# Hybrid decoder step: the first feed-forward block on its own, totals two blocks ahead, a fifth PSUM bank

## The chip, the cores and the metric

The kernel runs on one core of a Trainium2 chip. The metric is the time of one execution on the device in microseconds (us), as the median of three runs; a profile of one further execution shows where its time goes. Engines are TensorE (PE, with PEld for its weight loads), VectorE (DVE), ScalarE (ACT), GpSimd (POOL) and the queue that starts the loads (SP). Each engine works through its own queue in order; semaphores tie them together.

## The reference, cut to what matters

One inference step of a one-layer recurrent decoder for 256 prompt tokens and 8 x 4 sample tokens, 288 columns in all, with the width D = 2048. Three mixers run in parallel (RG-LRU, GLA, mLSTM), then an output projection; what the change touches is behind it:

```python
sh1, sc1, gt1, sh2, sc2, gt2 = [m[:, None, :] for m in jnp.split(mod, 6, axis=-1)]
...
x = x + gt1 * mix                                  # mix = merged @ P['w_out']
xn = rmsnorm(x, P['g_norm2']) * (1.0 + sc2) + sh2  # the second norm
x = x + gt2 * (jnp.square(jax.nn.relu(xn @ P['w_ff1'])) @ P['w_ff2'])
...
y = rmsnorm(x, g_final)
```

`w_ff1` is 2048 x 8192 and `w_ff2` 8192 x 2048, both f32. All tensors are f32.

## The kernel before, in words

Activations lie feature-major: 16 tiles of 128 features by 288 columns. The weights are streamed from HBM in pieces of 128 x 1024 f32 (512 KB).

**Feed-forward.** The hidden width is cut into 8 parts `hb`. A part takes four blocks of the first layer (`ff1`, weight `wf1`, two PSUM banks each) and four of the second (`ff2`, weight `wf2`, four banks each, summed up over the parts in `facc`, that is slots 6 and 7). `ff2(hb - 1)` follows `ff1(hb)`. A block has four pieces `g`, and each piece costs TensorE 24 matmuls: the f32 weight is split into two f16 halves, hi and lo, the activation likewise, and three of the four products are summed. So FF has 64 blocks, 256 steps `s` (one piece each) and 6144 matmuls.

The split needs a power of two for each block, so that f16 holds the halves. For a piece and a block (`class Block`):

- `fetch(i)` starts the load of piece `i` into one of 11 places. A place is free again when the piece that lay there is converted.
- `scan` squares the piece on ScalarE and sums it (L229, output to a scrap tile `con`, the sum in `sums`).
- `total` (one small TensorE matmul, L233, into a bank `px`) and `scale` (five tiny VectorE instructions, L198 to L201 and L238) make the power of two out of the block's four sums.
- `convert` writes hi, on ScalarE for the pieces listed in `by_act` (L242), else on VectorE (L244), and lo always on VectorE (L245). Both go to a tile `pair`, of which there are six.
- `multiply` issues the matmuls (L256). In a block's last piece they go bank by bank, and behind each bank stands its `evac`: in `ff1` a relu and a square on ScalarE (L1852, L1853); in `ff2` one VectorE instruction that adds the bank to `facc` (L1867), a copy on ScalarE for the first part, and in the last two parts also the gated residual (`resid`, L1757 to L1762). What reads a bank last sets it free; the pool `pm` has four.

`hidden_rows`, `hidden_total` and `hidden_part` do the same split for the hidden activations of a part: a total on TensorE, and four pairs of a ScalarE (L1844) and a VectorE instruction (L1845).

**What sets the order.** `feed_forward` writes the order out by hand, and `in_order` fixes it on TensorE, ScalarE and VectorE. Step `s` scans piece `s + 8`, scales the next block if `s % 4` is 1, converts piece `s + 3`, fetches `s + 14`, multiplies `s`, and issues the next block's total if `s % 4` is 0. Ahead of step 0 it fetches 11 pieces and scans 8. The first eight pieces belong to two blocks taken in turn, so that each norm tile serves twice as many matmuls. What stands outside `in_order` is placed by a scheduler.

**The second norm.** The output projection's last block ends with `resid` and the squares for the norm (L592); `scaled` multiplies x by the conditioning scale on GpSimd (slots `xf`), and `rstd_of` forms the reciprocal root (L601 on TensorE, L622 to L626 on VectorE with L624 on ScalarE). Then come 16 norm tiles `k`, outside `in_order`: the product with the root (L1813, VectorE), hi by ScalarE (L1814 for the prompt columns, L1817 for the sample columns), the sample columns' shift and lo (L1816, L1819, GpSimd from the third tile on), and lo for the prompt (L1818, VectorE). They use two row buffers in turn.

Beside the feed-forward, conditioning weights (`wada`) for `gt2` are prepared and multiplied (L404 to L412, and L426 on TensorE); `every` says at which steps.

Of the kernel before, what the change touches and what calls it, by code (L numbers as in the profile page):

```python
# [14 lines left out]
P = 128  # L15
D = 2048
KT = D // P
NP = 256
# [36 lines left out]
def trunk(ctx, tc, io):  # L55
# [151 lines left out]
    def in_order():  # L207
# [4 lines left out]
        for i in traced[n:]:  # L212
# [3 lines left out]
            if i.engine in (mybir.EngineType.PE, mybir.EngineType.Activation, mybir.EngineType.DVE):  # L216
                queued[i.engine] = i

    class Block:

        def __init__(self, w, blk, g0, width, act, back, evac, by_act):
# [24 lines left out]

        def multiply(self, g, hi, lo, ms, kks):
            if self.ps is None:
                self.ps = [pm.tile([P, 512], F32, tag="mm", name=nm("mm")) for _ in range(self.nm_t)]
            hi, lo = (t_.rearrange("p (k m) -> p k m", k=self.kg) for t_ in (hi, lo))  # L250
            for m in ms:
                for kk in kks:
                    k = self.kg * g + kk
                    xh, xl = self.act(k)
                    for i, (a, x) in enumerate(((hi, xh), (hi, xl), (lo, xh))):
                        pace["last"] = T.matmul(self.ps[m][:, :N], a[:, kk, m * P:(m + 1) * P], x, start=k == 0 and i == 0,  # L256
                                                stop=k == 4 * self.kg - 1 and i == 2)
# [1544 lines left out]
                scaled(i)  # L1802
        run(stream(io["wout"], b, act_m, KT, ev_o))
    every("")
    scaled(3)
    rs = rstd_of(pss)
    x16 = big.tile([P, 2, KT, N], F16, tag="xh", name="x16")
    with tc.high_priority():
        for k in range(KT):
            f = row(("ar", "mr")[k % 2])  # L1810
            E = V if k < 2 else G
            h, l, sh = x16[:, 0, k, :], x16[:, 1, k, :], mod[:, SH2, k, 0:1]
            V.tensor_tensor(out=f, in0=xf[k // 8][:, k % 8, :], in1=rs, op=ALU.mult)  # L1813
            S.activation(h[:, 0:NP], f[:, 0:NP], AF.Identity, bias=sh)  # L1814
            fs = f[:, NP:N].rearrange("p (b t) -> p b t", b=NB)
            E.tensor_tensor(out=fs, in0=fs, in1=mod[:, SH2, k, 1:9].unsqueeze(2).to_broadcast([P, NB, TS]), op=ALU.add)  # L1816
            S.activation(h[:, NP:N], f[:, NP:N], AF.Copy)  # L1817
            V.scalar_tensor_tensor(l[:, 0:NP], f[:, 0:NP], sh, h[:, 0:NP], ALU.add, ALU.subtract)  # L1818
            E.tensor_tensor(out=l[:, NP:N], in0=f[:, NP:N], in1=h[:, NP:N], op=ALU.subtract)  # L1819


    facc = (slot(6), slot(7))
    pss = None

    h = slot(2)
    hx = [big.tile([P, 2, 8, N], F16, tag=f"s{i}", name=nm("hx")) for i in range(2)]
# [20 lines left out]
    def ff1(hb):  # L1847
        for b in range(4):
            def ev(m, p, c, b=b):
                i = 2 * b + m  # L1850
                r = t288()
                S.activation(r, p, AF.Relu, scale=c)  # L1852
                S.activation(h[:, i, :], r, AF.Square, accum_out=hof[hb % 2][:, 8 + i:9 + i])  # L1853
            yield Block(io["wf1"], 4 * hb + b, 0, 256, lambda k: (x16[:, 0, k, :], x16[:, 1, k, :]), lambda: xback, ev, (1,))

    def ff2(hb):
        x = hx[hb % 2]
        for b in range(4):
            def ev(m, p, c, b=b):
                k = 4 * b + m  # L1860
                a = facc[k // 8][:, k % 8, :]
                if hb == 0:
                    S.activation(a, p, AF.Copy, scale=c)
                    return
                x = x2[k // 8][:, k % 8, :]
                if hb < 7:
                    V.scalar_tensor_tensor(a, p, c, a, ALU.mult, ALU.add)  # L1867
# [10 lines left out]
            yield Block(io["wf2"], b, 4 * hb, 512, lambda k: (x[:, 0, k, :], x[:, 1, k, :]), lambda: hback[hb][0], ev, (0, 1, 2))  # L1878

    blocks, after = [], {}  # L1880
    for hb in range(9):
        if hb < 8:
# [16 lines left out]
    def fetch(i):  # L1899
        if i >= total:  # L1900
            return
        j = i % 11
        if j < 2:
            t = big8[:, 1024 * j:1024 * j + 1024]
        elif j < 6:
            t = bigx[:, 1024 * (j - 2):1024 * (j - 1)]
        elif j < 9:
            t = wp.tile([P, 1024], F32, tag="raw", name=nm("raw"), bufs=3)
        else:
            t = big3[:, 1024 * (j - 9):1024 * (j - 8)]  # L1910
        b, g = order[i]
        Q.dma_start(t, b.w[b.blk, b.g0 + g])
        raws[i] = t
# [13 lines left out]
    def multiply(s):  # L1927
        b, g = order[s]
        ms, kks = range(b.nm_t), range(b.kg)
        if s < 8:  # L1930
            if s % 2 == 0:
                for kk in kks:
                    for i in (s, s + 1):
                        order[i][0].multiply(order[i][1], *pairs[i], ms, (kk,))
        elif g < 3:
            b.multiply(g, *pairs[s], ms, kks)
        else:
            for m in ms:
                b.multiply(g, *pairs[s], (m,), kks)
                b.evac(m, b.ps[m][:, :N], b.c)  # L1940
        if s in (6, 7):
            for m in ms:
                b.evac(m, b.ps[m][:, :N], b.c)
        del pairs[s]

    def feed_forward():

        with in_order():
            for i in range(11):
                fetch(i)  # L1950
            for i in range(8):
                scan(i)
                if i > 5:
                    blocks[i - 6].total()
                    blocks[i - 6].scale()
            for i in range(3):
                convert(i)
                fetch(11 + i)
        for s in range(total):
            if s == total - 33:  # L1960
                drain("gt1")
            if s == total - 16:
                tail.update(pss=longp(), ssum=row("gc"))
            b = s // 4 + 1
# [12 lines left out]

    slots.update(ids=(9, None, "st"), n=0)
    high.update(ids=(None,))
# [130 lines left out]
```

## Time and profile before

| | |
|---|---|
| median of three runs | 1926.03 us (1923.81 to 1926.28) |
| the profiled execution | 1925.75 us, span 1924.0 us |
| TensorE busy | 1850.7 us, 96% of the span |
| VectorE, ScalarE, GpSimd busy | 1280.6 us (67%), 1114.8 us (58%), 178.1 us (9%) |
| mean granted TensorE clock | 0.992 |
| HBM traffic | 403.56 MB read, 218 GB/s read and written over the span |
| feed-forward on TensorE | 1110.33 us to about 1910 us |

A row of a timeline gives the start in the span, the length, the engine, the line of the kernel and the operation with its tiles, then how often, and in brackets the idle time before it with what ended it. Rows of waits give who waited for whom, the sum, the number and the longest. Windows give the busy time of each engine named, the granted clock as a share of full speed, the share of the DMA engines that was busy, and GB/s. TensorE's matmuls overlap, so a group of them appears some 0.15 us longer than the distance to the next one.

### The profile page before, as it was taken

The numbers are of one execution on the slowest core, as the hardware profiler recorded it, in microseconds if no ns is written. First come the engines' busy times: TensorE is split into PE (matmuls) and PEld (weight loads), VectorE is DVE, ScalarE is ACT, GpSimd is POOL, SyncE is SP. The second block draws the span as 40 slices with busy tenths as digits, with TensorE's granted clock in tenths as the row PEclk, the third lists the DMA queues.
The fourth block names the chain that finished last, engine by engine and source line by source line (L and its number), as shares of the span: only waits on it lengthen the run. The fifth ranks groups of instructions, "written<-read, shape, count | busy, mean of one in ns | idle before, by whom it ended". The sixth has DMA issues, their size and how long they took to land.

```text
span 1924.0 us, 38831 instructions
## 1 busy us (share of the span) xinstructions
PE 1850.7 (96%) x15874; PEld 1622.3 (84%) x15874; DVE 1280.6 (67%) x2290; ACT 1114.8 (58%) x1861; POOL 178.1 (9%) x251
## 2 busy tenths in 40 slices
PE   8999999999999999999999789998999999999987
PEld 7998888999999999999999667777777777777765
DVE  4677746545684457776468578666867776767686
ACT  5333464445455344566367468967777767575654
POOL 0002100001141000011110620000000000000002
PEclk9999999999999999999999989999999999999999
DMA  9998756547744369856796665574565555555441
GB/s 386 399 369 309 249 200 235 208 156 275 253 155 163 134 202 309 295 184 238 285 358 255 249 241 183 160 249 145 173 211 183 165 187 164 187 164 188 145 130 50
DMA packets 113442, 422.90 MB, mean 220 GB/s; under 512 B 11808, under 2 KB 12096, under 8 KB 110064
## 3 DMA queue, kind: packets, MB, share of 16 engines
q1 hardware_dynamic: 97040, 361.04, 54.2%
q0 software_dynamic: 11472, 42.79, 6.4%
q10 hardware_dynamic: 4752, 16.60, 2.1%
q8 instruction: 124, 2.03, 0.4%
q14 instruction: 54, 0.44, 0.1%
HBM read 403.56 MB, written 16.81 MB: 218 GB/s over the span
## 4 chain that ended last, share of the span: by engine, by line
PE 75%; DVE 11%; ACT 9%; issue 3%; DMA 2%; SPq 0%; DVEq 0%; POOL 0%; ACTq 0%; POOLq 0%
PE mm L169 39%; PE mm L256 25%; ACT con L229 4%; PE pa L365 3%; DVE pair L245 3%; ACT pair L242 2%; PE px L169 2%; DVE lo L162 1%; DVE s L1867 1%; DMA raw<-win 1%; DVE pair L244 1%; DVE s L1757 1%; PE pa L426 1%; ACT hi L160 0%; DVE s L793 0%
## 5 line engine op out<-in xcount | busy, mean ns | idle before, releaser
L256 PEld LDWEIGHTS <-pair 128*128 128x128 f16 x6144 | 597.7, 98 | 192.9 <-issue 34.6
L160 ACT ACTIVATE hi<-raw 128x1024 fp32r<-128x1024 f32 x272 | 287.0, 1057 | 411.7 <-PE mm L169 254.5
L162 DVE TENSOR_TENSOR lo<-raw,hi 128x1024 fp32r<-128x1024 f32 x272 | 334.9, 1233 | 250.5 <-ACT hi L160 229.3
L169 PE MATMUL mm<-xh,hi 128*128 128x288 f32 x1440 | 428.8, 301 | 4.0 <-ACT xh L711 1.6
L169 PE MATMUL mm<-xl,hi 128*128 128x288 f32 x1440 | 423.4, 297 | 0.0
L169 PE MATMUL mm<-xh,lo 128*128 128x288 f32 x1440 | 412.3, 296 | 2.0 <-DVE lo L162 1.9
L256 PE MATMUL mm<-hx,pair 128*128 128x288 f16 x3072 | 386.2, 287 | 27.5 <-DVE s L1867 21.5
L256 PE MATMUL mm<-x,pair 128*128 128x288 f16 x3072 | 381.8, 287 | 4.2 <-DVE pair L244 2.5
L169 PEld LDWEIGHTS mm<-xh,hi 128*128 128x128 f32 x1440 | 269.9, 188 | 15.8 <-issue 8.1
L169 PEld LDWEIGHTS mm<-xl,hi 128*128 128x128 f32 x1440 | 270.3, 188 | 1.4
L169 PEld LDWEIGHTS mm<-xh,lo 128*128 128x128 f32 x1440 | 266.2, 188 | 4.9 <-DVE lo L162 2.9
L169 PE MATMUL mm<-s,hi 128*128 128x288 f32 x1280 | 254.1, 298 | 1.1 <-DVE s L1762 0.7
L169 PEld LDWEIGHTS mm<-s,hi 128*128 128x128 f32 x1280 | 203.2, 189 | 5.2 <-issue 2.9
L169 PE MATMUL mm<-s,lo 128*128 128x288 f32 x640 | 179.9, 297 | 1.6 <-DVE lo L162 1.0
L245 DVE SCALAR_TENSOR_TENSOR pair<-s,sums,pair 128x1024 f16<-128x1024 f32 x94 | 120.5, 1288 | 38.5 <-ACT pair L242 37.2
L245 DVE SCALAR_TENSOR_TENSOR pair<-xl,sums,pair 128x1024 f16<-128x1024 f32 x93 | 119.5, 1291 | 30.5 <-ACT pair L242 29.1
L169 PEld LDWEIGHTS mm<-s,lo 128*128 128x128 f32 x640 | 117.6, 189 | 2.3 <-DVE lo L162 2.1
L245 DVE SCALAR_TENSOR_TENSOR pair<-raw,sums,pair 128x1024 f16<-128x1024 f32 x69 | 88.3, 1283 | 27.9 <-ACT pair L242 26.9
L229 ACT ACTIVATE con<-s 128x1024 bf16<-128x1024 f32 x94 | 98.4, 1047 | 6.2 <-DMA s<-wf 5.2
L229 ACT ACTIVATE con<-xl 128x1024 bf16<-128x1024 f32 x93 | 97.2, 1046 | 3.2 <-DMA xl<-wf 2.3
L1852 ACT ACTIVATE t<-mm,sums 128x288 f32<-128x288 f32 x64 | 31.8, 498 | 89.6 <-PE mm L256 89.6
L610 POOL TENSOR_TENSOR row<-row,t 128x288 f32<-128x288 f32 x11 | 12.7, 1153 | 762.1 <-ACT t L608 761.5
(516 smaller groups left out, 2131.2 us busy)
## 6 DMA issues: line engine op xcount, KB each, us to landing
raw<-win SPq DMA_DIRECT2D x192, 512.0 KB, 4.6
s<-wf SPq DMA_DIRECT2D x94, 512.0 KB, 4.0
xl<-wf SPq DMA_DIRECT2D x93, 512.0 KB, 3.9
raw<-wf SPq DMA_DIRECT2D x69, 512.0 KB, 4.0
s<-wq SPq DMA_DIRECT2D x20, 1024.0 KB, 9.8
raw<-wout SPq DMA_DIRECT2D x32, 512.0 KB, 5.7
s<-wada SPq DMA_DIRECT2D x13, 1024.0 KB, 7.5
ag<-wada POOLq DMA_DIRECT2D x12, 1024.0 KB, 9.3
```

The lines of the kernel that those rows point to most:

```text
L160: pace["hi"] = S.activation(hi, raw, AF.Copy)
L162: pace["lo"] = V.tensor_tensor(out=lo, in0=raw, in1=hi.bitcast(F32), op=ALU.subtract)
L169: pace["last"] = T.matmul(ps, w[:, kk, ms], x, start=k == k0 and i == 0, stop=k == kt - 1 and i == 2)
L229: pace["hi"] = S.activation(junk, raw, AF.Square, accum_out=self.of[:, g:g + 1])
L242: pace["hi"] = S.activation(hi, raw, AF.Copy, scale=self.u)
L244: V.tensor_scalar(hi, raw, self.u, None, ALU.mult)
L245: pace["lo"] = V.scalar_tensor_tensor(lo, raw, self.u, hi, ALU.mult, ALU.subtract)
L256: pace["last"] = T.matmul(self.ps[m][:, :N], a[:, kk, m * P:(m + 1) * P], x, start=k == 0 and i == 0, stop=k == 4 * self.kg - 1 and i == 2)
L365: pace["prod"] = T.matmul(ps[32 * j:32 * j + 32, h * w // 4:(h + 1) * w // 4], stat(k), v[:, j], start=k == 0 and h == 0, stop=k == kt - 1 ...
L426: pace["prod"] = T.matmul(ps[32 * j:32 * j + 32, a:a + 256], c, v[:, j], start=q == i == n == 0, stop=q == KT // each - 1 and n == 1, skip ...
L1757: V.scalar_tensor_tensor(x[:, 0:NP], z[:, 0:NP], mod[:, kind, k, 0:1], x[:, 0:NP], ALU.mult, ALU.add)
L1852: S.activation(r, p, AF.Relu, scale=c)
```

## The change

It has five parts.

1. The first block runs alone. Its four pieces are loaded into places that the output projection leaves (three `raw` tiles and one `hi` tile), scanned, totalled and scaled ahead of the norm. The norm's tiles move into `feed_forward`, into `in_order`, four ahead of each of the first four steps, with a third row buffer, and three of the 16 products go to GpSimd.
2. From then on a step converts piece `s + 3` first, fetches `s + 14` and scans piece `s + 10`. The total of block `s // 4 + 2` is issued at `s % 4 == 2`; its scale stands where it stood, with the block's first conversion.
3. Other pieces are converted by ScalarE: `by_act` is (0,) for `ff1`, was (1,), and (0, 2, 3) for `ff2`, was (0, 1, 2). `hidden_part` comes one step later.
4. Every fifth bank is taken from the pool `pi`; the sum for the last norm moves to `pa`.
5. In the last part but one the residual is computed by GpSimd (`half_resid`), in three instructions a tile; VectorE only adds the bank to `facc`.

```diff
+    def bank():
+
+        taken["n"] += 1
+        return longp() if taken["n"] % 5 == 0 else pm.tile([P, 512], F32, tag="mm", name=nm("mm"))
...
-                self.ps = [pm.tile([P, 512], F32, tag="mm", name=nm("mm")) for _ in range(self.nm_t)]
+                self.ps = [bank() for _ in range(self.nm_t)]
...
-    with tc.high_priority():
-        for k in range(KT):
-            f = row(("ar", "mr")[k % 2])
...
+    def second_norm(k):
+
+        f = row(("ar", "mr", "gc")[k % 3])
+        E = V if k < 2 else G
+        h, l, sh = x16[:, 0, k, :], x16[:, 1, k, :], mod[:, SH2, k, 0:1]
+        (G if k % 4 == 3 and k < 15 else V).tensor_tensor(out=f, in0=xf[k // 8][:, k % 8, :], in1=rs, op=ALU.mult)
+        S.activation(h[:, 0:NP], f[:, 0:NP], AF.Identity, bias=sh)
...
+        V.scalar_tensor_tensor(l[:, 0:NP], f[:, 0:NP], sh, h[:, 0:NP], ALU.add, ALU.subtract)
...
-            yield Block(io["wf1"], 4 * hb + b, 0, 256, lambda k: (x16[:, 0, k, :], x16[:, 1, k, :]), lambda: xback, ev, (1,))
+            yield Block(io["wf1"], 4 * hb + b, 0, 256, lambda k: (x16[:, 0, k, :], x16[:, 1, k, :]), lambda: xback, ev, (0,))
+
+    def half_resid(x, a, k):
+
+        G.tensor_scalar(a[:, 0:NP], a[:, 0:NP], mod[:, GT2, k, 0:1], None, ALU.mult)
+        s = a[:, NP:N].rearrange("p (b t) -> p b t", b=NB)
+        G.tensor_tensor(out=s, in0=s, in1=mod[:, GT2, k, 1:9].unsqueeze(2).to_broadcast([P, NB, TS]), op=ALU.mult)
+        G.tensor_tensor(out=x, in0=x, in1=a, op=ALU.add)
...
-                        resid(x, a, GT2, k)
+                        half_resid(x, a, k)
...
-                after[s + 1 + 2 * i] = lambda hb=hb, i=i: hidden_part(hb, i)
+                after[s + 2 + 2 * i] = lambda hb=hb, i=i: hidden_part(hb, i)
...
-    order = [(blocks[i % 2], i // 2) for i in range(8)] + [(b, g) for b in blocks[2:] for g in range(4)]
+    order = [(b, g) for b in blocks for g in range(4)]
...
+        if i == 3:
+            t = wp.tile([P, 1024], F32, tag="hi", name=nm("raw"), bufs=3)
+        elif i < 4 or j > 7:
+            t = wp.tile([P, 1024], F32, tag="raw", name=nm("raw"), bufs=3)
...
+    first = {0: ((), (1,), ()), 1: ((4, 5), (2,), ()), 2: ((6, 7), (3,), (1,)), 3: ((8, 9), (4, 5, 6), ()),
+             4: ((10, 11, 12), (7,), ()), 5: ((13, 14, 15), (), (2,)), 6: ((16,), (8, 9), (3,))}
...
+            scans, converts, totals = first.get(s) or ((s + 10,), (s + 3,), (s // 4 + 2,) if s % 4 == 2 else ())
             with in_order():
-                scan(s + 8)
-                if s > 4 and s % 4 == 1 and b < len(blocks):
-                    blocks[b].scale()
-                convert(s + 3)
-                fetch(s + 14)
+                if s < 4:
+                    with tc.high_priority():
+                        for k in range(4 * s, 4 * s + 4):
+                            second_norm(k)
+                for i in converts:
+                    b, g = order[min(i, total - 1)]
+                    if g == 0 and i < total:
+                        b.scale()
+                    convert(i)
+                    fetch(i + 11)
+                for i in scans:
+                    scan(i)
                 multiply(s)
-                if s > 3 and s % 4 == 0 and b < len(blocks):
-                    blocks[b].total()
+                for b in totals:
+                    if b < len(blocks):
+                        blocks[b].total()
...
+    with in_order():
+        for i in range(4):
+            fetch(i)
+        for i in range(4):
+            scan(i)
+        for i in range(4, 12):
+            fetch(i)
+        blocks[0].total()
+        blocks[0].scale()
+        convert(0)
+    scaled(3)
+    rs = rstd_of(pss)
```

The table `first` gives, for the first seven steps, the pieces to scan, the pieces to convert and the blocks to total.

How the engines' queues change is shown at three places. In the rows a tile's number tells one buffer from another; `s`, `xl` and `raw` are places of loaded pieces, `row` the norm's row buffers, `x` (left of the arrow) the normed activations.

ScalarE at the end of the output projection, before: the last conversions of `wout`, the four squares for the norm, the table for the root, then a first scan.

```order
L160 ACTIVATE hi_12541<-raw_12540 128x1024
L592 ACTIVATE t_1748_12556<-s_1535_11145 128x288
...
L592 ACTIVATE t_1756_12631<-s_1535_11145 128x288
L1788 ACT_TABLE_LOAD
L1788 ACTIVATE warm_12560<-row_11151 128x1
L229 ACTIVATE con,sums_12815<-s_1783_12798 128x1024
L624 ACTIVATE rsc_12674<-t_1758_12672,eps 128x9
L229 ACTIVATE con,sums_12817<-s_1783_12798 128x1024
L1814 ACTIVATE x_12678<-row_12679,mod 128x256
L1814 ACTIVATE x_12678<-row_12686,mod 128x256
```

After:

```order
L160 ACTIVATE hi_12541<-raw_12540 128x1024
L236 ACTIVATE con,sums_12683<-raw_12675 128x1024
...
L236 ACTIVATE con,sums_12683<-raw_12681 128x1024
L599 ACTIVATE t_1748_12556<-s_1535_11145 128x288
...
L1795 ACTIVATE warm_12560<-row_11151 128x1
L249 ACTIVATE pair_12703<-raw_12675,sums_12683 128x1024
L631 ACTIVATE rsc_12714<-t_1773_12712,eps 128x9
L1821 ACTIVATE x_12666<-row_12718,mod 128x256
```

The four scans of the first block (now L236) stand ahead of the squares, and its first conversion ahead of the root; the scans that stood among the norm's tiles are gone from there.

VectorE in the norm, before, from the third tile on: products (L1813) and lo (L1818).

```order
L1813 TENSOR_TENSOR row_12693<-s_1713_12300,row_12671 128x288
L1813 TENSOR_TENSOR row_12700<-s_1713_12300,row_12671 128x288
L452 TENSOR_TENSOR mod<-t_1802_12909,par 128x72
L1818 SCALAR_TENSOR_TENSOR x_12678<-row_12693,mod,x_12678 128x256
L1818 SCALAR_TENSOR_TENSOR x_12678<-row_12700,mod,x_12678 128x256
L1813 TENSOR_TENSOR row_12707<-s_1713_12300,row_12671 128x288
L1813 TENSOR_TENSOR row_12714<-s_1713_12300,row_12671 128x288
```

After, from the third tile on, with the product now L1820 and lo L1825:

```order
L1820 TENSOR_TENSOR row_12732<-s_1713_12300,row_12711 128x288
L1825 SCALAR_TENSOR_TENSOR x_12666<-row_12732,mod,x_12666 128x256
L1825 SCALAR_TENSOR_TENSOR x_12666<-row_12739,mod,x_12666 128x256
L251 TENSOR_SCALAR pair_12746<-raw_12677,sums_12683 128x1024
L252 SCALAR_TENSOR_TENSOR pair_12746<-raw_12677,sums_12683,pair_12746 128x1024
L1820 TENSOR_TENSOR row_12780<-s_1713_12300,row_12711 128x288
L1825 SCALAR_TENSOR_TENSOR x_12666<-row_12780,mod,x_12666 128x256
L1820 TENSOR_TENSOR row_12787<-s_1713_12300,row_12711 128x288
L1825 SCALAR_TENSOR_TENSOR x_12666<-row_12787,mod,x_12666 128x256
```

Each lo follows its own product at once, a conversion stands behind every four tiles, and the fourth tile's product is GpSimd's.

TensorE within the second layer, before: a block's first piece ends, the total of the next block (`px`, from `sums_15305`), the second piece; and, 72 matmuls behind the total, the first use of its scale.

```order
L256 MATMUL mm_15461<-hx_12795,pair_15347 128x288
L233 LDWEIGHTS ones
L233 MATMUL px_15486<-sums_15305,ones 128x4
L256 LDWEIGHTS pair_15379
L256 MATMUL mm_15458<-hx_12795,pair_15379 128x288
...
L256 LDWEIGHTS pair_15494
```

After: a block's third piece ends, the total of the block after next, the fourth piece; the first use of that scale is 120 matmuls behind the total.

```order
L263 MATMUL mm_15320<-hx_12669,pair_15276 128x288
L240 LDWEIGHTS ones
L240 MATMUL px_15411<-sums_15242,ones 128x4
L263 LDWEIGHTS pair_15312
L263 MATMUL pi_15317<-hx_12669,pair_15312 128x288
...
L263 LDWEIGHTS pair_15496
```

The total moved two pieces forward, and one bank in five is now `pi`.

More of the change, by code (lines that the diff above doesn't have):

```diff
@@ L1877, in ev @@
                     S.activation(x, x, AF.Copy, scale=Pm("gf")[:, k:k + 1])
-            yield Block(io["wf2"], b, 4 * hb, 512, lambda k: (x[:, 0, k, :], x[:, 1, k, :]), lambda: hback[hb][0], ev, (0, 1, 2))
+            yield Block(io["wf2"], b, 4 * hb, 512, lambda k: (x[:, 0, k, :], x[:, 1, k, :]), lambda: hback[hb][0], ev, (0, 2, 3))
     blocks, after = [], {}
@@ L1906, in fetch @@
             t = bigx[:, 1024 * (j - 2):1024 * (j - 1)]
-        elif j < 9:
-            t = wp.tile([P, 1024], F32, tag="raw", name=nm("raw"), bufs=3)
         else:
-            t = big3[:, 1024 * (j - 9):1024 * (j - 8)]
+            t = big3[:, 1024 * (j - 6):1024 * (j - 5)]
         b, g = order[i]
@@ L1929, in multiply @@
         ms, kks = range(b.nm_t), range(b.kg)
[L1930 to L1934, printed above, removed]
+        if s < 4:
+            for kk in kks:
+                b.multiply(g, *pairs[s], ms, (kk,))
         elif g < 3:
             b.multiply(g, *pairs[s], ms, kks)
-        else:
-            for m in ms:
+        for m in ms if g == 3 else ():
+            if s > 3:
                 b.multiply(g, *pairs[s], (m,), kks)
[L1940 to L1943, printed above, removed]
+            b.evac(m, b.ps[m][:, :N], b.c)
         del pairs[s]
+    first = {0: ((), (1,), ()), 1: ((4, 5), (2,), ()), 2: ((6, 7), (3,), (1,)), 3: ((8, 9), (4, 5, 6), ()),
+             4: ((10, 11, 12), (7,), ()), 5: ((13, 14, 15), (), (2,)), 6: ((16,), (8, 9), (3,))}
     def feed_forward():
[L1948 to L1958, printed above, removed]
         for s in range(total):
```

29 lines of the change are left out of this document (12 added, 17 removed).

## Prediction

> **What bounds the kernel now.** I read the page's busy shares first, then the chain that ended last, TensorE's waits, its timeline, and last the timelines of VectorE and ScalarE where it waits.
>
> ```profile
> PE 1850.7 (96%) x15874; PEld 1622.3 (84%) x15874; DVE 1280.6 (67%) x2290; ACT 1114.8 (58%) x1861; POOL 178.1 (9%) x251
> ...
> 1165.55 11.78 PE mm L256 x96
> ...
> PE mm L256 <- DVE s L1867: 21.7, 26, 2.5
> PE mm L256 <- ACT s L1863: 3.1, 3, 1.3
> PE mm L256 <- DVE rs_t L1760: 2.8, 2, 1.6
> ...
> 1110.33 0.66 PE L256 MATMUL mm<-x,pair 128*128 128x288 f16 x2 [2.52 <-DVE pair L244]
> 1114.15 18.76 PE L256 MATMUL mm<-x,pair 128*128 128x288 f16 x136 [0.63 <-DVE pair L245]
> 1254.74 0.29 PE L426 MATMUL pa<-uh,uc 128*32 128x256 f16 x4
> ...
> 1553.33 0.28 PE L426 MATMUL pa<-ag,uc 128*32 128x256 f16 x4
> 1802.55 0.17 PE L233 MATMUL px<-sums,ones 128*128 128x4 bf16 x1
> 1802.58 0.36 PE L1837 MATMUL px<-hs,ones 128*128 128x1 f32 x2
> 1802.80 8.98 PE L256 MATMUL mm<-hx,pair 128*128 128x288 f16 x72
> 1813.03 0.90 PE L256 MATMUL mm<-hx,pair 128*128 128x288 f16 x6 [1.25 <-DVE s L1867]
> 1814.31 0.90 PE L256 MATMUL mm<-hx,pair 128*128 128x288 f16 x6 [0.38 <-DVE s L1867]
> 1909.78 0.65 PE L616 MATMUL pi<-row,ones 128*128 128x288 f32 x2
> ```
>
> The first row is the page's: TensorE (PE) is busy 96% of the span. The chain's row (start, length) is a block of the feed-forward (FF) at full rate: 96 matmuls in 11.78 us, 0.1227 us each, 2.95 us for a step of 24. The next three are TensorE's waits from 1080 us on (total, times, longest). The rest is its timeline: FF begins at 1110.33, and the row that follows its last matmul starts at 1909.78, so it takes 799.4 us, where 6144 matmuls at 0.1227 would take 753.9. The 45.5 us between is what can be won there, and I split it.
>
> (a) The start. Eight matmuls, then 136 in one run, end at 1132.91: 22.6 us for work of 17.7, so 4.9 are lost.
>
> (b) Work that stays: 32 conditioning rows such as those of 1254.74 and 1553.33, 0.11 us apart (3.5 us), and eight totals like that of 1802.58, 0.22 us to the next row (1.8).
>
> (c) The rest, 35.3 us, are the seams between blocks of the second layer (wf2). The three waits add up to 27.6 us in 31 times. A wait costs more than it reports: the rows of 1813.03 and 1814.31 start 1.28 us apart for six matmuls worth 0.74, a loss of 0.54 for 0.38 reported. 31 x 0.16 is 5.0 more, 32.6 in all; I take 34 us as the stake.
>
> Why a seam stalls is seen on VectorE (DVE) and ScalarE (ACT) ahead of the wait of 1813.03; the last two rows are windows, with VectorE's and ScalarE's busy time in the third and fourth figure:
>
> ```profile
> 1804.53 1.28 DVE L245 SCALAR_TENSOR_TENSOR pair<-raw,sums,pair 128x1024 f16<-128x1024 f32 x1 [0.96 <-ACT pair L242]
> 1811.26 1.28 DVE L245 SCALAR_TENSOR_TENSOR pair<-s,sums,pair 128x1024 f16<-128x1024 f32 x1 [0.79 <-ACT pair L242]
> 1812.46 0.51 DVE L1867 SCALAR_TENSOR_TENSOR s<-mm,sums,s 128x288 f32<-128x288 f32 x1
> 1813.74 0.51 DVE L1867 SCALAR_TENSOR_TENSOR s<-mm,sums,s 128x288 f32<-128x288 f32 x1
> ...
> 1803.35 1.15 ACT L242 ACTIVATE pair<-raw,sums 128x1024 f16<-128x1024 f32 x1
> 1806.30 0.78 ACT L1844 ACTIVATE hx<-s,hs 128x576 f16<-128x576 f32 x1 [1.80 <-DVE hs L200]
> 1811.80 1.04 ACT L229 ACTIVATE con<-xl 128x1024 bf16<-128x1024 f32 x1
> ...
> 1200.00:1260.00 60.00, 56.90 (x503) 44.94 (x501) 42.68 (x70) 50.76 (x89) 0.00 (x0) 1.00 0.54 170
> 1310.00:1360.00 50.00, 44.50 (x365) 35.15 (x364) 37.84 (x70) 39.09 (x63) 0.00 (x0) 1.00 0.48 153
> ```
>
> The next block's scale starts from a total that TensorE computes at 1802.55. Only then, at 1803.35, can ScalarE convert the next block's first tile; two more follow, with scans and hidden tiles between them in its queue (one of which waits 1.80 us itself). VectorE's lo of the third, at 1811.26, has waited 0.79 us for ScalarE, and the release of the bank (1812.46) stands behind it in VectorE's queue. TensorE had finished that bank's sum at 1802.80 + 54 x 0.1227 = 1809.4, 3 us earlier. So a late scale holds the bank. Load doesn't: where the waits are longest (1310 to 1360, 5.5 us idle) the two are busy 37.84 and 39.09 of 50 us.
>
> **The change, part by part.** *Earlier totals, scans ten ahead, other tiles by ScalarE.* The order shows 120 matmuls (14.7 us) between a total and the first use of its scale, against 72 (8.8 us). The chain above then begins 5.9 us earlier, twice what the release was late. Taking the idle out of a window leaves ScalarE 39.09 of 44.5 us, and in the worst one 50.76 of 56.9, 89%: little room, but not over. Expected: most of the 34.
>
> *Fifth bank.* A seam's first sum now has a free bank, and the release of the block's first bank is needed six matmuls, 0.74 us, later. That alone takes 0.74 from each wait.
>
> *Residual on GpSimd.* In the last pass but one VectorE's step from release to release is 1813.74 - 1812.46 = 1.28 us, most of it residual; it leaves VectorE. GpSimd (POOL) gets three instructions for each of 16 tiles.
>
> ```profile
> 1066.02 6.23 POOL L1770 TENSOR_SCALAR s<-s,mod 128x256 f32<-128x256 f32 x4
> 1875.19 2.93 POOL L610 TENSOR_TENSOR row<-row,t 128x288 f32<-128x288 f32 x2 [0.17 <-ACT t L608]
> ...
> 1875.77 1.70 DVE L245 SCALAR_TENSOR_TENSOR pair<-xl,sums,pair 128x1024 f16<-128x1024 f32 x1
> ```
>
> By these rows a 256-column product takes 1.6 us and a 288-column sum 1.5 beside VectorE; with a short one, some 3.3 us a tile, 53 in all, off the path, since the last pass needs each tile only four blocks (47 us) later and takes them one by one. The price is on VectorE: its lo took 1.70 us beside GpSimd's sums, against 1.28 at 1811.26, 1.7 us a block of four. In a block that VectorE fills to 0.85 (37.84 of 44.5, 10.0 of 11.78) this makes 11.7: it may just bind. I charge 1 us; bounds 0 and 4 x 1.7 = 7.
>
> *First block alone, norm tiles in its queues.* Its four loads take places that are free once the output projection's last tiles are converted, its scans stand where ScalarE had nothing to do, so its scale is known before the norm. TensorE can begin at the first norm tile, about 1096, not at 1110. But the order shows VectorE alternating product and lo of one tile, where two tiles were interleaved before.
>
> ```profile
> 1094.76 0.83 DVE L1813 TENSOR_TENSOR row<-s,row 128x288 f32<-128x288 f32 x2
> 1095.86 0.88 DVE L1818 SCALAR_TENSOR_TENSOR x<-row,mod,x 128x256 f16<-128x256 f32 x2
> 1109.53 0.74 DVE L244 TENSOR_SCALAR pair<-s,sums 128x1024 f16<-128x1024 f32 x1
> ...
> 1095.32 0.91 ACT L1814 ACTIVATE x<-row,mod 128x256 f16<-128x256 f32 x2 [0.16 <-DVE row L1813]
> ...
> 1000.00:1003.00 3.00, 1.63 (x7) 0.84 0.10 15
> 1003.00:1006.00 3.00, 3.00 (x16) 0.59 0.95 340
> 1101.00:1104.00 3.00, 0.00 (x0) 0.51 1.03 421
> 1116.00:1119.00 3.00, 3.00 (x18) 0.65 0.85 270
> ```
>
> Product at 1094.76, ScalarE's half at 1095.32, lo at 1095.86: 1.10 us from product to lo, the next product 0.4 (a lo of 0.88 / 2) behind, 1.5 us a tile. A step of 24 matmuls has four tiles, one of them with its product on GpSimd in the first three steps (0.7), and a conversion, 0.74 + 1.28 less overlap, 1.9: 3 x 1.5 + 0.7 + 1.9 = 7.1 us, where TensorE needs 2.95. The first step costs about 0.4 more for its sample columns. From 1094.7 on, 7.5 + 7.1 + 7.1, then 4 x 1.5 = 6.0, is 1122.4. The second block's scale (0.6), hi (1.15) and lo (1.28) come behind that, so step 4 runs from about 1125.5, with 98 matmuls done. Before, 144 - (1132.91 - 1125.5) / 0.1227 = 84 were done by then: the change is 14 ahead, 1.7 us.
>
> Off that goes the clock. The windows (busy, granted clock) show it halved after TensorE's 6 us without work in 1101 and full again within 1116 to 1119, about 4 us into the unbroken run; and in 1000 to 1003 two waits and 1.63 us of work were enough to lose it. The stutter has 0.74 us of work in 1.5, so I charge one such loss, 3.5 us at half speed, 1.75. The start comes to 0. Bounds: +9 (tiles at 0.8 us, as two interleaved need: 0.83 / 2 and 0.88 / 2) and -8 (a conflict with GpSimd of 0.5 us a tile).
>
> The Trainium skill (TensorE: Matmul & The Clock Gate, HAM oscillation) asks only that TensorE never idle for more than some 3.4 us. By it the stutter's gaps (an estimate: 1.9 + 1.5 less 0.74 of work, 2.7 us at most) cost no clock, and the sum would be 1893; the windows of 1000 to 1006 speak against it, and I go by them.
>
> *Loads.* A scan now has three loads under way behind it, not five.
>
> ```profile
> s<-wf SPq DMA_DIRECT2D x94, 512.0 KB, 4.0
> ...
> ACT con L229 <- DMA s<-wf: 1.9, 2, 1.5
> ```
>
> A load lands in 4.0 us, and three steps are 8.8, so I cost it at nothing; what hides it is that margin. ScalarE waited 1.9 us for such loads after 1110.
>
> **Sum.** Start 0, seams -34, left over +3 (GpSimd's conflict 1, the blocks in which ScalarE is at 89% 2): -31 us. The profiled execution took 1925.75 (span 1924.0), so 1895; the three runs' median, 1926.03, lies 0.3 above. A difference under 0.2% (4 us) can't be told from none.
>
> **Rivals.** *The start gains too:* if VectorE's tiles overlap after all, 9 us more, 1886. For it: VectorE's own time is under 0.9 us a tile. Against: the order.
>
> *Only the bank helps:* ScalarE has as much to do as before and stays the late one. Then 0.74 comes off each wait; those of 0.38 vanish, those of 1.25 keep 0.5, the longest (2.5) 1.8. About 13 of the 34 remain: 1905.
>
> *Slower: scans starve.* If loads land late, a scan waits, ScalarE's queue behind it, then the total in TensorE's own queue. One us a block over 64 blocks is +64, with the seams' -31 1959; from 0.5 us a block on it decides. The 1.9 us above speak against it.
>
> *The stalls only move:* TensorE waits for totals instead of banks, 1926.
>
> **Chances.** Forecast 0.62 (its own range 1888 to 1902), the start gains too 0.12, only the bank 0.13, a start 8 us or more worse with the seams gone 0.06 (1903 to 1911), starving 0.05, moved 0.02. 1884 to 1909 leaves out the last two, half of the worse start and a little of the first rival. Faster 0.93, same 0.02, slower 0.05.
>
> **What would show it.** Right: waits on wf2's release under 5 us in all; a pass of wf2 in about 47.5 us; VectorE's norm products some 1.5 us apart, and about 100 matmuls done at 1125. Wrong: conversions on ScalarE still waiting for VectorE's sums, scans waiting for loads, norm tiles at 0.8 us, or the clock at half after 1130.

## The result, and the profile after

The changed kernel takes 1895.97 us (median; 1895.02 to 1896.28) against 1925.16 us for the kernel before in the same comparison: a ratio of 0.985, 95% interval 0.983 to 0.987. The forecast was 1895 us. The profiled execution takes 1895.68 us, its span 1893.9, 30.1 less than the span before. The number came out; the account behind it did only in part.

Three views of the changed kernel follow: the busy shares of the page, TensorE's waits from 1130 us on (sum, number, longest), and rows of its timeline. The line numbers are those of the changed kernel, 7 higher up to the norm and 3 to 10 higher behind it (L263 was L256, L240 was L233, L249 was L242, L1877 was L1867).

```profile
PE 1847.8 (98%) x15874; PEld 1621.6 (86%) x15874; DVE 1268.2 (67%) x2239; ACT 1117.3 (59%) x1861; POOL 219.9 (12%) x302
```

```profile
PE pi L263 <- DVE rs_t L1767: 1.8, 1, 1.8
PE mm L263 <- ACT s L1873: 1.4, 2, 0.7
PE px L240 <- ACT con L236: 1.4, 2, 1.0
PE pi L263 <- DVE s L1877: 1.4, 3, 1.0
PE mm L263 <- DVE s L1877: 1.3, 5, 0.6
```

```profile
1084.70 1.93 PE L372 MATMUL pa<-xh,silc 128*32 128x256 f32 x32
1122.94 5.81 PE L263 MATMUL mm<-x,pair 128*128 128x288 f16 x46 [0.90 <-DVE pair L252]
1132.70 0.16 PE L240 MATMUL px<-sums,ones 128*128 128x4 bf16 x1 [0.98 <-ACT con L236]
1206.50 2.37 PE L263 MATMUL mm<-hx,pair 128*128 128x288 f16 x18
1687.91 2.37 PE L263 MATMUL mm<-hx,pair 128*128 128x288 f16 x18
1735.52 8.98 PE L263 MATMUL mm<-x,pair 128*128 128x288 f16 x72
1879.70 0.65 PE L623 MATMUL pa<-row,ones 128*128 128x288 f32 x2
```

Two more rows of the kernel before are needed: its first conditioning matmul behind the output projection, and the first matmul of wf2.

```profile
1086.24 1.94 PE L365 MATMUL pa<-xh,silc 128*32 128x256 f32 x32
1209.58 3.10 PE L256 MATMUL mm<-hx,pair 128*128 128x288 f16 x24
```

From them the 30.1 us are split:

- Ahead of the change: the conditioning matmul starts at 1084.70 instead of 1086.24, 1.54 us earlier. That is within what it varies by: in two experiments that alter only the feed-forward (g1, f2) it stands at 1083.41 and 1088.40.
- The start, from there to the first matmul of wf2: 1206.50 - 1084.70 = 121.80, was 1209.58 - 1086.24 = 123.34. It gained 1.54.
- The rest of FF: 1879.70 - 1206.50 = 673.20, was 1909.78 - 1209.58 = 700.20. It gained 27.0, all of it in wf2: the six wf1 passes in it take 47.1 us (one 48.7) in both. What follows FF is 14.2 in both.

The release waits in wf2 (all but the third of the five) are 5.9 us in all, were 27.6. A pass with one wait of 0.17 takes 1735.52 - 1687.91 = 47.6; three of the eight passes take that, the others 48 to 51. The prediction had named under 5 us of waits and a pass of about 47.5.

### The profile page after: what moved, and what is told of

Same layout as the page of the kernel before. It is cut to its first block, busy times and chain, and to the rows that moved or that the text cites. A ratio compares the mean times of both kernels' runs of the same rounds, so it can differ in the third digit from the quotient of the medians.

```text
span 1893.9 us, 38893 instructions
## 1 busy us (share of the span) xinstructions
PE 1847.8 (98%) x15874; PEld 1621.6 (86%) x15874; DVE 1268.2 (67%) x2239; ACT 1117.3 (59%) x1861; POOL 219.9 (12%) x302
## 4 chain that ended last, share of the span: by engine, by line
PE 80%; DVE 9%; ACT 6%; issue 3%; DMA 1%; POOL 0%; SPq 0%; DVEq 0%; ACTq 0%; POOLq 0%
PE mm L169 39%; PE mm L263 24%; PE pi L263 6%; PE pa L372 3%; DVE pair L252 2%; ACT pair L249 2%; PE px L169 2%; DVE lo L162 1%; ACT con L236 1%; DMA raw<-win 1%; ACT hi L160 1%; PE pa L433 1%; DVE pair L251 0%; DVE s L800 0%; PE px L1649 0%
## 5 line engine op out<-in xcount | busy, mean ns | idle before, releaser
L263 PEld LDWEIGHTS <-pair 128*128 128x128 f16 x6144 | 596.6, 98 | 176.8 <-issue 11.9
L263 PE MATMUL mm<-x,pair 128*128 128x288 f16 x2448 | 316.1, 287 | 10.1 <-ACT x L1824 6.3
L263 PE MATMUL mm<-hx,pair 128*128 128x288 f16 x2472 | 321.8, 286 | 2.7 <-ACT s L1873 1.4
L252 DVE SCALAR_TENSOR_TENSOR pair<-raw,sums,pair 128x1024 f16<-128x1024 f32 x72 | 93.2, 1295 | 41.6 <-ACT pair L249 40.6
L1861 POOL TENSOR_SCALAR s<-s,mod 128x256 f32<-128x256 f32 x16 | 21.5, 1347 | 675.7 <-DVE s L1877 675.7
L236 ACT ACTIVATE con<-s 128x1024 bf16<-128x1024 f32 x92 | 96.3, 1046 | 1.3 <-DMA s<-wf 0.3
L236 ACT ACTIVATE con<-xl 128x1024 bf16<-128x1024 f32 x92 | 96.2, 1046 | 0.9
L263 PE MATMUL pi<-hx,pair 128*128 128x288 f16 x600 | 89.8, 286 | 3.1 <-DVE rs_t L1767 1.8
```

Source lines behind the costliest of these rows:

```text
L236: pace["hi"] = S.activation(junk, raw, AF.Square, accum_out=self.of[:, g:g + 1])
L252: pace["lo"] = V.scalar_tensor_tensor(lo, raw, self.u, hi, ALU.mult, ALU.subtract)
L1861: G.tensor_scalar(a[:, 0:NP], a[:, 0:NP], mod[:, GT2, k, 0:1], None, ALU.mult)
```

## The experiments

Ratios, with the 95% interval, are to runs of the kernel before on the same chip. The last two are from the traces, as in the split above: the start, from the first conditioning matmul to the first matmul of wf2, and the rest of FF. They are free of what varies ahead of FF, but each is one execution, and executions of one kernel differed by 0.5 to 6 us. So the ratios put f1's gain at 7.7 us, where its trace has 5.7 (start and rest), the cost of e3 at 8.9, not 6.4, and that of g2 at 18.9, not 20.9.

| kernel | median, us | ratio to before | start | rest |
|---|---|---|---|---|
| before | 1925.16 | 1 | 123.3 | 700.2 |
| changed | 1895.97 | 0.9848 (0.9831 to 0.9865) | 121.8 | 673.2 |
| e1, changed, four banks | 1901.33 | 0.9880 (0.9865 to 0.9895) | 122.3 | 679.3 |
| e2, changed, late totals | 1896.65 | 0.9853 (0.9837 to 0.9870) | 121.1 | 674.5 |
| e3, changed, residual on VectorE | 1903.99 | 0.9894 (0.9879 to 0.9908) | 121.8 | 679.6 |
| e4, changed, old tiles for ScalarE | 1892.34 | 0.9833 (0.9819 to 0.9848) | 121.6 | 669.8 |
| f1, before, fifth bank | 1917.97 | 0.9960 (0.9948 to 0.9973) | 123.2 | 694.7 |
| f2, before, early totals | 1922.58 | 0.9987 (0.9978 to 0.9996) | 123.4 | 698.2 |
| f3, start and scans alone | 1912.60 | 0.9929 (0.9916 to 0.9943) | 120.3 | 690.3 |
| f4, changed, norm in pairs | 1892.85 | 0.9828 (0.9815 to 0.9841) | 118.8 | 673.1 |
| g1, before, scan behind | 1916.12 | 0.9961 (0.9949 to 0.9974) | 123.3 | 693.3 |
| g2, changed, scan first | 1913.94 | 0.9946 (0.9933 to 0.9960) | 122.2 | 693.7 |
| g3, changed, pairs and old tiles | 1891.44 | 0.9827 (0.9814 to 0.9841) | 118.7 | 670.3 |
| g4, before, three edits | 1900.57 | 0.9877 (0.9863 to 0.9890) | 122.7 | 676.3 |

**e1, four banks.**

```diff
-        return longp() if taken["n"] % 5 == 0 else pm.tile([P, 512], F32, tag="mm", name=nm("mm"))
+        return pm.tile([P, 512], F32, tag="mm", name=nm("mm"))
```

> The changed kernel with the fifth bank taken back: every sum of the feed-forward comes from the four mm banks. Theory A (a late scale held the banks; the total is now early enough): a seam loses at most the 0.74 us that the fifth bank gives, and mostly nothing, since the chain starts 5.9 us earlier and the release was 3 us late: 1896 to 1899 us. Theory B (the bank did the work, ScalarE stays the late one): about 0.74 us in each of the 31 waits comes back, 20 us or more: 1916.

1901.33: 6.1 us of the rest come back. Neither theory gave that. The bank is worth something and far from all.

**e2, late totals.**

```diff
-             4: ((10, 11, 12), (7,), ()), 5: ((13, 14, 15), (), (2,)), 6: ((16,), (8, 9), (3,))}
+             4: ((10, 11, 12), (7,), ()), 5: ((13, 14, 15), (), (2,)), 6: ((16,), (8, 9), ())}
...
-            scans, converts, totals = first.get(s) or ((s + 10,), (s + 3,), (s // 4 + 2,) if s % 4 == 2 else ())
+            scans, converts, totals = first.get(s) or ((s + 10,), (s + 3,), (s // 4 + 1,) if s % 4 == 0 else ())
```

> The changed kernel with each block's total back at its old place, one step before the scale, 72 matmuls ahead of its first use instead of 120; scans, banks, residual and start as changed. Theory A: the late scale comes back and the bank takes 0.74 us off each wait, so some 13 of the 34 us return: 1905 to 1909. If the bank counts for nothing beside it, 1915 to 1921. Theory B (the bank alone): 1896 to 1898.

1896.65, 1.3 us in the rest. This takes away the predicted cause almost without effect: theory A falls, at least as the main part.

**e3, residual on VectorE.**

```diff
-                        half_resid(x, a, k)
+                        resid(x, a, GT2, k)
```

> The changed kernel with the residual of the last pass but one back on VectorE. That pass took 58.1 us before and 48.0 in the changed kernel, against 49 to 50 for its neighbours before. Theory A (the scale was late everywhere, in this pass too): VectorE has 0.77 us more in each of 16 tiles, 3.1 us a block of 11.8 in which it is busy some 10: about 1 us a block returns, 1900, bounds 1896 and 1905. Rival C (the residual alone made that pass long): 8 to 9 us return, 1905. Rival D (GpSimd's sums cost VectorE more than they save): 1894 or less.

1903.99: 6.4 us in the rest, all of it in the last two passes of wf2 (103.5 us, were 97.0 in the changed kernel). That lies between A's 4 us and rival C's 8 to 9; by the ratios (8.9) it fits C. Either way GpSimd's part is a large gain, not a small cost.

**e4, old tiles for ScalarE.**

```diff
-            yield Block(io["wf1"], 4 * hb + b, 0, 256, lambda k: (x16[:, 0, k, :], x16[:, 1, k, :]), lambda: xback, ev, (0,))
+            yield Block(io["wf1"], 4 * hb + b, 0, 256, lambda k: (x16[:, 0, k, :], x16[:, 1, k, :]), lambda: xback, ev, (1,))
...
-            yield Block(io["wf2"], b, 4 * hb, 512, lambda k: (x[:, 0, k, :], x[:, 1, k, :]), lambda: hback[hb][0], ev, (0, 2, 3))
+            yield Block(io["wf2"], b, 4 * hb, 512, lambda k: (x[:, 0, k, :], x[:, 1, k, :]), lambda: hback[hb][0], ev, (0, 1, 2))
```

> The changed kernel with the old choice of the tiles that ScalarE converts: the second of a first-layer block, the first three of a second-layer block. The number of tiles on each engine is the same, only the place moves. Theory A: within 2 us of the changed kernel, 1895 to 1898, since the scale is early enough for either. Rival E (the third tile in ScalarE's queue was what came late before the release): 4 us or more return, 1900 to 1906.

1892.34: 3.4 us less in the rest, a sign that no theory had. By the traces this part of the change costs time (2.8 us between f4 and g3 too); by the ratios it is 2.9, with intervals that overlap, and 0.2 between f4 and g3.

**f1, the fifth bank alone.** The edit is `bank()` of the change, put into the kernel before, with the last norm's sum in `pa`.

> The kernel before with the fifth bank alone (the final norm's sums take another bank, so that one stays free). Theory A: the bank takes 0.74 us from each of 31 waits, of which about 13 of 34 us stay: 1904 to 1908 us. Theory B (only the bank helps): the same or better, 1900. Theory F (releases come one by one in VectorE's queue, so one more bank moves the wait and does not shorten it): 1918 to 1925.

1917.97, at the edge of theory F's range: 5.5 us in the rest. Why a bank does so little is seen in the second part, where the waits are longest. VectorE's release rows and TensorE's wait, of the kernel before and then of f1:

```profile
1323.14 1.79 DVE L1867 SCALAR_TENSOR_TENSOR s<-mm,sums,s 128x288 f32<-128x288 f32 x4
1337.59 1.79 DVE L1867 SCALAR_TENSOR_TENSOR s<-mm,sums,s 128x288 f32<-128x288 f32 x4
1338.15 3.10 PE L256 MATMUL mm<-hx,pair 128*128 128x288 f16 x24 [2.50 <-DVE s L1867]
```

```profile
1322.71 1.79 DVE L1873 SCALAR_TENSOR_TENSOR s<-mm,sums,s 128x288 f32<-128x288 f32 x4
1337.15 0.51 DVE L1873 SCALAR_TENSOR_TENSOR s<-pi,sums,s 128x288 f32<-128x288 f32 x1
1337.72 0.90 PE L262 MATMUL pi<-hx,pair 128*128 128x288 f16 x6 [2.50 <-DVE s L1873]
```

From one block's release to the next it takes 14.45 us before and 14.44 with the bank, where TensorE needs 11.8. The wait is 2.50 both times. Here ScalarE and VectorE set the block's time, one behind the other: after the release of 1323.14 VectorE has the second instruction of a hidden tile (L1845), a hi, a conditioning product (L412) and a lo in its queue ahead of the scale (1328.72), ScalarE's next hi (1329.34) waits 3.30 us for that scale, and the next release stands behind that hi and two more. A further bank is a lead that can be used up once, not a shorter loop: the wait one block earlier, 2.33 before, is 1.59 in f1, 0.74 less, and the next one is as long as it was.

**f2, early totals alone.**

```diff
-                scan(s + 8)
+                for i in (8, 9) if s == 0 else (s + 9,):
+                    scan(i)
...
-                if s > 3 and s % 4 == 0 and b < len(blocks):
-                    blocks[b].total()
+                if s % 4 == 2 and b + 1 < len(blocks):
+                    blocks[b + 1].total()
```

> The kernel before with scans nine ahead instead of eight and each block's total two steps earlier (120 matmuls ahead of its first use instead of 72), with four banks, the residual on VectorE, the old choice of ScalarE's tiles and the old start. Theory A: most of the seams' 26 us goes, except in the last pass but one where VectorE has the residual: 1898 to 1904. Theory B (the bank does the work): 1921 to 1925.

1922.58, 2.0 us in the rest. Theory A falls from this side too.

**f3, the start and the scans alone.** The edits of e1 to e4 together.

> The changed kernel with fifth bank, early totals, GpSimd residual and ScalarE's tiles all taken back, so that of the change only the start and the scans ten ahead are left. The traces give the start 2.8 us, and the work ahead of it ended 1.5 us earlier, which may be chance or the change's: 1921 to 1923 if the two traces are read rightly. As predicted (start 0): 1925. If the seams gain from the scans ten ahead alone: under 1915.

1912.60, under the 1915 that was named for a gain from the scans. The start gives 3.0, the rest 9.9. What is left of the change in the steady steps is the lead of ten, the hidden tiles one step later, and one thing that the prediction had not priced: a step now converts first and scans afterwards.

**f4, the norm in pairs.**

```diff
-                        for k in range(4 * s, 4 * s + 4):
+                        for k in (4 * s, 4 * s + 2):
                             second_norm(k)
```

with `second_norm` writing both products, then both of ScalarE's halves, then both lo's.

> The changed kernel with the second norm's tiles emitted in pairs: both products, then both of ScalarE's halves, then both lo's. A step of four tiles took 7.1 us with VectorE busy about two thirds of it, since each lo waits for ScalarE. Theory G (that serial chain sets the start): a pair takes about 2 us instead of 3, a step about 5: four steps bring 4 to 8 us, 1888 to 1892. Rival H (ScalarE's scans, which stand behind the norm's tiles, are late next; one total waited 0.98 us for them): 0 to 2 us, 1894 to 1896.

1892.85, between the two: the start takes 3.0 us less, so the alternation of product and lo cost at least that.

**g1, the scan behind the conversion, alone.**

```diff
-                scan(s + 8)
                 if s > 4 and s % 4 == 1 and b < len(blocks):
                     blocks[b].scale()
                 convert(s + 3)
                 fetch(s + 14)
+                scan(s + 8)
```

> The kernel before with one line moved: in each step the scan of a later tile stands behind the scale and the conversion in ScalarE's queue, not ahead of them; eight ahead as before. Theory J (the scan, 1.2 us on ScalarE, stood ahead of the hi that the seam waits for; the kernel with the start alone, in which this order had changed too, took 10.1 us less for the eight wf2 passes): 1913 to 1917. Rival K (the two more tiles of lead did that): 1923 to 1926.

1916.12, as theory J says: one moved line gives 6.9 us in the rest. Its mechanism is in the rows of the sixth part's first seam. In the kernel before, ScalarE (hidden tile, scan, hi, scan, hi), then VectorE's last lo and the release, then TensorE's wait:

```profile
1709.92 0.78 ACT L1844 ACTIVATE hx<-s,hs 128x576 f16<-128x576 f32 x1 [1.80 <-DVE hs L200]
1710.60 1.04 ACT L229 ACTIVATE con<-xl 128x1024 bf16<-128x1024 f32 x1
1711.64 1.13 ACT L242 ACTIVATE pair<-s,sums 128x1024 f16<-128x1024 f32 x1
1712.68 1.04 ACT L229 ACTIVATE con<-xl 128x1024 bf16<-128x1024 f32 x1
1713.72 1.13 ACT L242 ACTIVATE pair<-s,sums 128x1024 f16<-128x1024 f32 x1
1714.89 1.28 DVE L245 SCALAR_TENSOR_TENSOR pair<-s,sums,pair 128x1024 f16<-128x1024 f32 x1 [0.80 <-ACT pair L242]
1716.09 1.78 DVE L1867 SCALAR_TENSOR_TENSOR s<-mm,sums,s 128x288 f32<-128x288 f32 x4
1716.65 3.10 PE L256 MATMUL mm<-hx,pair 128*128 128x288 f16 x24 [1.25 <-DVE s L1867]
```

The same of g1:

```profile
1702.82 0.77 ACT L1844 ACTIVATE hx<-s,hs 128x576 f16<-128x576 f32 x1 [0.76 <-DVE hs L200]
1703.50 1.13 ACT L242 ACTIVATE pair<-s,sums 128x1024 f16<-128x1024 f32 x1
1704.54 1.04 ACT L229 ACTIVATE con<-xl 128x1024 bf16<-128x1024 f32 x1
1705.58 1.13 ACT L242 ACTIVATE pair<-s,sums 128x1024 f16<-128x1024 f32 x1
1706.74 1.28 DVE L245 SCALAR_TENSOR_TENSOR pair<-s,sums,pair 128x1024 f16<-128x1024 f32 x1 [0.79 <-ACT pair L242]
1707.95 1.79 DVE L1867 SCALAR_TENSOR_TENSOR s<-mm,sums,s 128x288 f32<-128x288 f32 x4
1708.51 3.10 PE L256 MATMUL mm<-hx,pair 128*128 128x288 f16 x24 [0.22 <-DVE s L1867]
```

From the hidden tile to the release it is 6.17 us before and 5.13 in g1: one scan of 1.04 less, and the wait falls from 1.25 to 0.22. The hi that the release needs does not wait for the scale there; it stands behind scans in ScalarE's queue, and behind VectorE's hidden scale.

**g2, the scan first again, in the changed kernel.**

```diff
+                if s > 6:
+                    for i in scans:
+                        scan(i)
                 for i in converts:
...
-                for i in scans:
-                    scan(i)
+                if s < 7:
+                    for i in scans:
+                        scan(i)
```

> The changed kernel with the scan put ahead of the conversions again from step 7 on, still ten ahead. Theory J: the seams lose what the order gave, 5 to 10 us (fifth bank and residual cover a part): 1901 to 1906. Rival K: 1896 to 1898.

1913.94, past theory J's range: 20.5 us of the rest come back. The same place in g2 (hidden total on TensorE, the hidden tile on ScalarE, the release on VectorE, TensorE's wait, and an undisturbed run of as many matmuls), then two windows of g2 behind such waits, then the place in the changed kernel:

```profile
1703.51 0.28 PE L1840 MATMUL px<-hs,ones 128*128 128x1 f32 x2
1710.98 0.78 ACT L1847 ACTIVATE hx<-s,hs 128x576 f16<-128x576 f32 x1 [2.74 <-DVE hs L200]
1715.07 1.36 DVE L1877 SCALAR_TENSOR_TENSOR s<-mm,sums,s 128x288 f32<-128x288 f32 x3
1715.63 9.92 PE L263 MATMUL mm<-hx,pair 128*128 128x288 f16 x66 [2.25 <-DVE s L1877]
1220.28 8.24 PE L263 MATMUL mm<-hx,pair 128*128 128x288 f16 x66 [0.88 <-ACT s L1873]
```

```profile
1420.00:1423.00 3.00, 2.28 (x19) 1.83 (x19) 3.00 (x6) 2.70 (x4) 0.00 (x0) 1.00 0.56 187
1617.00:1620.00 3.00, 2.87 (x13) 1.85 (x13) 3.00 (x6) 2.12 (x4) 0.00 (x0) 0.56 0.55 175
```

```profile
1690.86 0.28 PE L1840 MATMUL px<-hs,ones 128*128 128x1 f32 x2
1697.29 0.78 ACT L1847 ACTIVATE hx<-s,hs 128x576 f16<-128x576 f32 x1 [1.56 <-DVE hs L200]
1700.34 1.36 DVE L1877 SCALAR_TENSOR_TENSOR s<-mm,sums,s 128x288 f32<-128x288 f32 x3
```

From the hidden total to the release it is 11.56 us in g2 and 9.48 in the changed kernel: 2.08, the length of the two scans that now stand ahead of conversions. The wait is 2.25, and it is paid twice: the 66 matmuls behind it take 9.92 us, where 66 take 8.24 in the second row, 1.7 more, because the granted clock falls. This happened behind five of the six waits of over 2 us (five of 2.24 or 2.25, one of 3.42).

**g3, pairs and old tiles.** The edits of f4 and e4 together, on the changed kernel.

> The changed kernel with the norm's tiles in pairs and the old choice of ScalarE's tiles. They lie in different stages (start: 3.1 us, seams: 3.7), so the sum should hold: 1889, within 1. If the earlier start only moves a wait into the first blocks, 1892.

1891.44 by the median, not to be told from e4 or f4. In the trace both gains are there (118.7 and 670.3, together 6.1 us less than the changed kernel), so it is the best version by its trace and no worse than the others by its time.

**g4, three edits on the kernel before.** The edits of f1 and g1, and the residual of the change.

> The kernel before with three edits alone: the scan behind the conversion, the fifth bank, the residual of the last pass but one on GpSimd. Totals, lead of the scans, ScalarE's tiles and start as before. If these three are the seams' whole gain (wf2 passes 415.8 before; 405.7 with the order; 385.4 with all but the other tiles for ScalarE): some 28 to 30 us less than before, 1895 to 1897. If the early totals are needed beside them: 1900 or more (the single prices, 10 + 7 + 8, would give 1900).

1900.57, where the prices in the expectation lead: the rest is 676.3, 23.9 of the 27.0. The prices measured here are lower, 6.9 and 5.5 alone and 6.4 when undone, 18.8 together, so the three gain more together than one by one. Scan order, bank and GpSimd carry the seams. All the rest of the change there, the totals, the lead, the tiles and the later hidden tiles, brings the last 3; the lead and the later hidden tiles were not run alone.

## Why the prediction was right, and where it was not

**The start: right in its steps, wrong in the clock.** Of the changed kernel, VectorE's products, TensorE's runs, and windows (the clock is the third figure from the end):

```profile
1092.53 0.46 DVE L1820 TENSOR_TENSOR row<-s,row 128x288 f32<-128x288 f32 x1
1099.85 0.45 DVE L1820 TENSOR_TENSOR row<-s,row 128x288 f32<-128x288 f32 x1
1101.28 0.50 DVE L1820 TENSOR_TENSOR row<-s,row 128x288 f32<-128x288 f32 x1
1102.86 0.49 DVE L1820 TENSOR_TENSOR row<-s,row 128x288 f32<-128x288 f32 x1
...
1101.02 0.28 PE L263 MATMUL mm<-x,pair 128*128 128x288 f16 x1 [1.99 <-ACT x L1824]
1117.07 3.74 PE L263 MATMUL mm<-x,pair 128*128 128x288 f16 x17 [0.17 <-POOL x L1826]
1121.62 0.42 PE L263 MATMUL mm<-x,pair 128*128 128x288 f16 x2 [0.81 <-ACT pair L249]
```

```profile
1102.00:1105.00 3.00, 2.17 (x11) 1.14 (x9) 1.96 (x5) 2.17 (x7) 2.49 (x7) 0.67 1.02 406
1117.00:1120.00 3.00, 2.93 (x12) 1.67 (x13) 1.81 (x6) 1.25 (x4) 1.35 (x5) 0.50 0.00 0
```

The products stand 1.5 us apart, and 98 matmuls are done 30.4 us behind the first (1122.94); 1.5 and 30.8 were predicted. The clock was lost, at 0.67 and 0.50. It cost nothing, though I charged 1.75: TensorE's slow run of 3.74 ends at 1120.8, and the next step still waits 0.81 for ScalarE. By my own sum VectorE set the start, and a loss on an engine that waits anyway has no price. The clock is back (1.00 in 1123 to 1126) before the long run: its 46 matmuls take 5.81 us. Then a total waits 0.98 us (1132.70) for scans, and 1.54 remain; 0 was predicted.

The Trainium skill (TensorE: Matmul & The Clock Gate, HAM oscillation) asks for no gap over some 3.4 us. Its sum charged no loss, and in time there was none; but the clock itself fell here with no gap over the 1.99 us of the row of 1101.02, and in g2 waits of 2.25 were enough. These runs do not bear that bound out.

**Earlier totals, "most of the 34": the step that failed.** They measure 2.0 alone and 1.3 when undone. The chain that I quoted was read from its first link. The total did come late at 1802.55, but the first hi (1803.35) stood behind two scans as well (1801.12 and 1802.28), which ended only as the scale was there. Behind the hidden tile of 1806.30, ScalarE's queue in the kernel before ran scan, hi, scan, hi:

```profile
1806.98 1.04 ACT L229 ACTIVATE con<-xl 128x1024 bf16<-128x1024 f32 x1
1808.02 1.13 ACT L242 ACTIVATE pair<-s,sums 128x1024 f16<-128x1024 f32 x1
1809.06 1.04 ACT L229 ACTIVATE con<-xl 128x1024 bf16<-128x1024 f32 x1
1810.10 1.13 ACT L242 ACTIVATE pair<-s,sums 128x1024 f16<-128x1024 f32 x1
```

Pulling the total forward shortens none of these. Ahead of the wait of 1338.15, where a scale did hold ScalarE (3.30 us, to 1329.34), its total was there at 1326.64, and it was VectorE's queue that came late. The prediction said that scans stood between and did not price their move, though the change puts every conversion ahead of its scan. This order measures 6.9 alone; undoing it costs 20.5, and five clock losses of 1.7 us make some 8 of these. Why the other 12 are more than 6.9 was not followed.

**Fifth bank, 0.74 off each wait:** 31 waits make 23 us; measured 5.5 and 6.1. The arithmetic held for single waits, not for a loop that is longer than TensorE's block. So the bank alone, which that rival puts at 1905, measured 1918 in f1.

**Residual, charged 1 net:** it gains 6.4. The sign was wrong because only the conflict was priced, while the gain stood unnamed in the 34. The conflict is real but short. In the changed kernel, while GpSimd does its first four sums (1802.00 to 1808.00), VectorE's lo at 1805.53 takes 1.81 us against 1.28, and the one ahead of it 1.70; TensorE's next wait for a release (1807.83) is 0.23. Later lo's beside GpSimd's sums (1819.51, 1831.30) take the usual 1.28, so one block paid, not four.

**Other tiles for ScalarE, costed with the totals:** they lose 3.4. VectorE's hi and lo of the second tile now stand ahead of the hidden scale in its queue; in e4, at the same seam, the hidden total comes at 1689.88 and the release at 1697.54, 7.66 us instead of 9.48. But TensorE's wait there was only 0.17, so this shows the order and little of the 3.4; most of it lies in the first pass of wf2 (51.1 us, 49.8 in e4) and the last two (97.0, 94.8), less what the second gives back (49.2, 50.5), and was not followed there.

**Loads, at nothing:** right. ScalarE waited once for one behind 1110 us, for 0.3 us.

**Left over, 3:** with 35.3 us at stake in the seams and 27.0 won, 8.3 are left. So the start was 1.5 better than forecast, the work ahead of it 1.5 by chance, and the seams 4 worse (27 for a net 31). The 1895 was right because the stake had been measured well, and because these three nearly cancel. That is luck: the cause on which most of the 34 rested brought about 2, and what brought the rest had no term of its own in the sum, or a wrong one.

## What to carry to other kernels

When a release is late, list everything that stands in the queue of each engine between the last event that was in time and the release, and price the change by what leaves that list: here two scans of 1.04 us mattered, and the input that came first did not. A buffer more helps once; it does not help where the loop of the other engines is longer than a block. Before charging a slower clock, ask whether the engine is the one that sets the end there.

## What the runs showed of the hardware that I had not expected

Waits of nearly one length had two outcomes for the clock. In g2, 2.25 us lost it behind 1715.63 and kept it in 1420 to 1423 (1.00). In the kernel before, behind the wait of 2.50 shown above, it stayed:

```profile
1338.00:1341.00 3.00, 2.85 (x24) 2.27 (x24) 2.96 (x7) 1.21 (x3) 0.00 (x0) 1.00 0.48 175
```

Shorter waits lost it in the same kernel: behind waits of 1.42 and, six matmuls later, 0.38 us, 18 matmuls from 1844.95 on took 4.04 us, where 18 take 2.37 at full clock, and the granted clock of 1845 to 1848 was 0.53. The length of one wait does not decide alone; what else does, no run here settles.
